# Shifting the moving operands of a decoder layer's matrix products by 48 bytes, and planning one small product later

## The chip, the cores and the metric

The kernel runs as one program on 1 core of one Trainium2 chip. The metric is the time of one execution on the device in microseconds (us), lower is better. The kernel before takes 1654.64 us, the median of 3 runs that lie between 1654.36 and 1654.86 us.

## What is computed

The reference is one layer of a decoder with three parallel branches. A prompt of 256 tokens and 8 samples of 4 tokens each pass through the same weights, so the kernel treats them together as T = 288 columns. Cut to what matters here:

```
h = rms_norm(x, g_mix);  proj = h @ w_in            # 2048 -> 10752 columns
u = u_lin * sigmoid(u_gate)                          # branch A: causal depthwise convolution, LayerNorm, swish
y_conv = swish(layer_norm(conv31(u))) @ w_conv_out
q, k = rms_norm(q_sb), rms_norm(k_sb)                # branch B: 8 heads of 128, stick-breaking attention
y_sb = stick_breaking(q, [past_k, k], [past_v, v]) @ w_sb_out
y_mem = softmax_attention(rms_norm(q_mem), mem_k, mem_v) @ w_mem_out    # branch M: 4 heads
x = x + (g_A*y_conv + g_B*y_sb + g_M*y_mem) @ w_o    # g_*: sigmoid gates out of proj
x = x + square(relu(rms_norm(x, g_mlp) @ w_up)) @ w_down                # 2048 -> 8192 -> 2048
```

All inputs are float32. The keys and values of the memory and of the new tokens are returned too.

## The kernel before

**Layout.** Activations lie with features on the 128 partitions and the 288 tokens along the free dimension, so a tensor of 2048 features is 16 tiles of 128x288. A weight is the stationary operand of a product, an activation tile the moving one, and a sum over the features builds up in one bank of PSUM (the memory into which TensorE writes).

**Three products for one.** The type `float32r` holds a rounded float32. To keep the precision, weights and activations are each split into a high part and a low part, both `float32r`: ScalarE (ACT) casts the weights (L302), VectorE (DVE) subtracts to get the low part (L313). One 128x128 block of weights then costs three products of 288 columns: high weight by high and by low activation, low weight by high activation. `products` (L490) writes them in pieces of 6; all go through `chunk` (L482), so nearly all of TensorE's work has the line L484. There are 11,712 such products, called *main products* here. The weights come in 504 slabs of 128x1024 floats (24 main products each) that SyncE's queue (SP) loads in order.

**Stages.** First the keys and values of the prompt's memory (`mem_products`, L537: there the weights are the moving operand, 512 columns wide), then the columns of `w_in` for the convolution (`conv_products`), the 4 memory heads, the 8 stick-breaking heads (key, query, value of each), gates and branch projections, `w_o`, and four rounds of `w_up` and `w_down`. Attention, convolution and the samples run on the other engines beside the main products, with small products of their own in between. The norms of a head need the sum of the squares over its 128 features: `head_norm` (L806) squares on ScalarE, adds the halves and splits on VectorE (L816, L820), and multiplies by a matrix of ones (L823). There are 20 such products. `sum_norm` (L443) does the same over 2048 features with two products (L439, L440).

**The order of the work.** Nothing is scheduled at run time. While the program is built, a planner (`Order`, L75) holds every step as an `Ask` with an engine, an estimated time, flags to wait for and buffers to take. It places the steps one by one at the earliest time it computes, by rank among those that are equally early. The estimates so set the order of the instructions in each engine's queue. `MM` (L176) is its estimate in us for one main product. `late` in an `Ask` puts a step that many us later than its inputs would allow. The engines then run their queues in that order and wait for semaphores.

**Where the operands lie.** The moving operands of the main products are in three pools. Pool `a` has 75 buffers of `APART` = 320 floats; an activation takes two of them, for its high and its low part (class `Acts`, L322), and uses the first 288 floats of each. From the fourth stage on, when the samples are done, the 9 buffers of `k4` (1024 floats, three operands in each, 320 apart) and the 8 of `s` (512 floats) become the fixed places of 16 operand pairs (`make_homes`, L1239). In the built program every one of the 11,712 moving operands starts 96 bytes past a multiple of 256; the blocks of weights start 32 bytes past a multiple of 64, and the weights that are moving operands at L537 also start 96 bytes past a multiple of 256. The convolution's first outputs lie in PSUM pools `pa` (3 banks) and `pm` (4 banks) and are held until the norm of x (`rx`, L434) is there.

Of the kernel before, what the change touches and what calls it, by code (L numbers as in the profile page):

```python
# [8 lines left out]
F32R = mybir.dt.float32r  # L9
# [5 lines left out]
P = 128  # L15
# [6 lines left out]
T = NP + NS  # L22
# [52 lines left out]
class Order:  # L75
# [31 lines left out]
    def give(self, pool, n=1):  # L107
        self.pools[pool] += [self.now.ready] * n
# [45 lines left out]
def dve(n, *flags, **take):  # L154
    return Ask("DVE", 0.18 + n / 920.0, flags, **take)


def act(n, *flags, **take):
    return Ask("ACT", 0.22 + n / 1200.0, flags, **take)
# [6 lines left out]
def pe(us, *flags, **take):  # L166
    return Ask("PE", us, flags, **take)


def sp(*flags, **take):  # L170
    return Ask("SP", 0.45, flags, **take)


APART = 320
VISIT, VISIT_K = 4, 8
MM = 0.1325  # L176
MM_MEM = 0.226


# [1 line left out]
def tile_decoder_step(ctx: ExitStack, tc: tile.TileContext, xT, memT, wall, cvec, kmat, ptab,  # L181
# [25 lines left out]
    def tl(p, shape, dt=F32):  # L207
        cnt[0] += 1
        return pools[p].tile(shape, dt, tag=p, name=f"{p}_{cnt[0]}")

    def bank(p):
        return tl(p, [P, 512])
# [46 lines left out]
    def col(c):  # L259
        return cv[:, c:c + 1]  # L260
# [9 lines left out]
    class Slab:  # L270
        def __init__(self, parts):
            self.parts = parts
            self.landed = [Flag() for _ in range(parts)]
            self.split = [Flag() for _ in range(parts)]
# [47 lines left out]
    class Acts:  # L322


        def __init__(self, n=T):
            self.h, self.l = tl("a", [P, APART], F32R)[:, :n], tl("a", [P, APART], F32R)[:, :n]
            self.flag = Flag()

    hm, hx = [None] * KT, [None] * KT
# [93 lines left out]
    def rsqrt_of(ss, n, dim, y, a, out):  # L423

        yield act(n)
        act_fn(LN_EXP, y, ss, AF.Ln, scale=1.0 / dim, bias=eps)
        yield act(n)
        act_fn(LN_EXP, y, y, AF.Exp, scale=-0.5)
        yield dve(n)
        nc.vector.scalar_tensor_tensor(a, ss, EPS * dim, y, op0=ALU.add, op1=ALU.mult)  # L430
        yield dve(n)
        nc.vector.scalar_tensor_tensor(a, a, -0.5 / dim, y, op0=ALU.mult, op1=ALU.mult)
        yield dve(n)
        nc.vector.scalar_tensor_tensor(out, a, 1.5, y, op0=ALU.add, op1=ALU.mult)  # L434

    def total(h, l, n):

        ss = bank("pa")[:, :n]
        nc.tensor.matmul(ss, ones_r, h, start=True, stop=False)  # L439
        nc.tensor.matmul(ss, ones_r, l, start=False, stop=True)  # L440
        return ss

    def sum_norm(acc, dim, out, flag, ready):  # L443
# [6 lines left out]
        nc.vector.tensor_sub(l, acc, h.bitcast(F32))  # L450
        yield pe(2 * MM, pa=1)
        ss = total(h, l, T)
# [37 lines left out]
    def products(ps, uses, acts, first=True, last=True, n=T):  # L490
# [6 lines left out]
        for i in range(0, len(todo), STEP):  # L497
            part = todo[i:i + STEP]
            yield pe(len(part) * MM, *sl.split, *{a.flag for _, _, a, _ in part})
            if i == 0 and first:  # L500
# [45 lines left out]
    def conv_products(evacs):  # L546
# [8 lines left out]
        for k2, o in turns:  # L555
# [9 lines left out]
            for i in range(2):  # L565
                todo.append((sl.l, slice(i * 512 + o * P, i * 512 + (o + 1) * P), "h", 2 * k2 + i))
            yield pe(6 * MM, *sl.split, hx_in[2 * k2], hx_in[2 * k2 + 1])
            if o == 0:
# [153 lines left out]
    def conv_norm():  # L722
# [7 lines left out]
        for turn in range(2):  # L730
# [5 lines left out]
            nc.vector.tensor_sub(l, acc, h.bitcast(F32))  # L736
            yield pe(2 * MM, pa=1)
            ss = total(h, l, T)
# [67 lines left out]
    def head_norm(ps, gcol, box, flag, p="pm"):  # L806

        yield dve(T, rx_done, t=4)
        raw, sq, hl, r = (tl("t", [P, T], F32R if i == 2 else F32) for i in range(4))
        nc.vector.tensor_mul(raw, ps, rx)  # L810
        give(p)
        yield act(T)
        nc.scalar.activation(sq, raw, AF.Square)
        yield dve(T)
        top, low = slice(0, P // 2), slice(P // 2, P)
        nc.vector.tensor_add(sq[top], sq[top], sq[low])  # L816
        yield act(T)
        nc.scalar.copy(hl[top], sq[top])
        yield dve(T)
        nc.vector.tensor_sub(hl[low], sq[top], hl[top].bitcast(F32))  # L820
        yield pe(MM, pa=1)
        ss = bank("pa")[:, :T]
        nc.tensor.matmul(ss, ones_r, hl, start=True, stop=True)  # L823
        yield from rsqrt_of(ss, T, HD, sq, r, r)
        give("pa")
        yield dve(T, a=1)
        out = tl("a", [P, T])
        nc.vector.scalar_tensor_tensor(out, raw, col(gcol), r, op0=ALU.mult, op1=ALU.mult)
        give("t", 4)
        box.append(out)  # L830
        done(flag)
# [45 lines left out]
    def mem_head(h):  # L877
        def evac(ps):
            box = []
            yield from head_norm(ps, C_GQM, box, Flag())  # L880
            q = box[0]
            if h == 0:
# [180 lines left out]
    def sb_key(h):  # L1063
        def evac(ps):
            box, ks[h] = [], Pair()
            yield from head_norm(ps, C_GK, box, Flag())
            add(store(oK[h], box[0]), 3)
            yield act(NS)
            nc.scalar.copy(kn[:, h, :], box[0][:, NP:])
            yield from split(ks[h], box[0][:, :NP], NP, k_made[h])  # L1070
            give("a")
        return evac

    def sb_query(h):
        def evac(ps):
            box, qs_[h] = [], Pair()
            yield from head_norm(ps, C_GQ, box, Flag())
            yield from split(qs_[h], box[0][:, :NP], NP, q_made[h])
            yield act(NS)
            nc.scalar.copy(qs[:, h, :], box[0][:, NP:])  # L1080
            give("a")
            done(qs_made[h])
        return evac
# [155 lines left out]
    def make_homes():  # L1239
        yield sp(*conv_done, *osb_in, k4=bufs["k4"], s=bufs["s"])  # L1240
        parts = []
        for _ in range(bufs["k4"]):
            x = tl("k4", [P, 1024], F32R)
            parts += [x[:, i * APART:i * APART + T] for i in range(3)]
        for _ in range(bufs["s"]):
            parts.append(tl("s", [P, 512], F32R)[:, :T])
        for j in range(KT):
            homes.append(Home(parts[2 * j], parts[2 * j + 1]))
        done(homes_in)
# [199 lines left out]
    with tc.manual_schedule():  # L1449
        add(loads(), 1.0)  # L1450
        add(cast_weights(), lambda: 0 if due(cast_at[0]) - order.free["ACT"] < 6.0 else 4.5)
        add(mem_norm(), 0.6)
        add(sum_norm(x_sum, D_MODEL, rx, rx_done, sums_x), 0.6)
        add(main(), 20.0)
        add(conv_norm(), 8.0)
        add(setup(), 1.0)
        add(read_pages(), 4.0)
        add(make_homes(), 1.0)
        order.run()
# [157 lines left out]
```

## Time and profile before

| | |
|---|---|
| median of 3 runs | 1654.64 us |
| the profiled execution | 1654.51 us |
| its span, first to last instruction | 1652.7 us |
| TensorE, matmuls (PE) | busy 1647.8 us, 12,786 instructions |
| TensorE, weight loads (PEld) | busy 1629.8 us |
| VectorE (DVE) | busy 991.7 us |
| ScalarE (ACT) | busy 737.8 us |
| GpSimd (POOL) | busy 140.1 us |
| DMA | 305.39 MB, mean 185 GB/s |

The profiled execution's own time is 1.8 us longer than its span and 0.13 us below the median. In a row of groups stand the line, the engine, the operation, the tiles (out<-in), shapes and count, then the busy time in us, the mean length of one in ns, and the idle time in front of them with what ended it. A matmul's length there is from its start to its end, and neighbours overlap, because they are pipelined; how fast they follow each other is read from the chain of waits, where a piece `849.22 800.29 PE pm L484 x6078` means: from 849.22 us on, for 800.29 us, 6078 matmuls one behind the other.

### The profile page before, as it was taken

To read this page: it belongs to the slowest core of one execution; us is meant where nothing else is said; L and a number is where in the kernel's file an instruction comes from. 1 tells how busy PE (TensorE), PEld (TensorE's weight loads), DVE (VectorE), ACT (ScalarE), POOL (GpSimd) and SP (SyncE) were. 2 spreads that over 40 slices of the span, in tenths; PEclk is the share of its full clock that TensorE was granted. 3 is DMA by queue.
4 is the path that set the end of the run, shared out by engine and by line. 5 is a ranking of instruction groups with operands and counts; after the bars stand their busy time and mean duration, and the time that the engine had idled before them with its cause. 6 is when DMAs were issued, how large, how long until landed. Compare 5 with 4: busy or idle time off the path is not lost.

```text
span 1652.7 us, 30966 instructions
## 1 busy us (share of the span) xinstructions
PE 1647.8 (100%) x12786; PEld 1629.8 (99%) x12786; DVE 991.7 (60%) x1471; ACT 737.8 (45%) x1070; POOL 140.1 (8%) x105
## 2 busy tenths in 40 slices
PE   9999999999999999999999999999999999999999
PEld 7999999999999999999999999999999999999999
DVE  7898888876677655565555544455444554455443
ACT  7846766644444534444443333333333333333332
POOL 0030000000000000001222200121001210022100
PEclk9999999999999999999999999999999999999999
DMA  9686466766755555546655555555555555555563
GB/s 326 221 182 250 140 206 206 263 244 232 259 163 165 169 172 167 170 153 208 188 173 166 167 167 166 167 166 170 165 171 166 168 167 166 166 166 166 178 189 100
DMA packets 107103, 305.39 MB, mean 185 GB/s; under 512 B 19922, under 2 KB 29522, under 8 KB 106962
## 3 DMA queue, kind: packets, MB, share of 16 engines
q1 hardware_dynamic: 106818, 303.39, 58.3%
q8 instruction: 100, 1.64, 0.4%
q14 instruction: 41, 0.34, 0.1%
q10 hardware_dynamic: 144, 0.02, 0.0%
HBM read 297.05 MB, written 6.32 MB: 184 GB/s over the span
## 4 chain that ended last, share of the span: by engine, by line
PE 99%; DVE 1%; issue 0%; POOL 0%; POOLq 0%
PE pm L484 92%; PE pm L537 3%; PE pa L484 1%; PE pl L1013 1%; PE pl L1186 0%; PE pa L850 0%; PE pa L851 0%; PE pa L849 0%; DVE a L715 0%; DVE wl L313 0%; PE pl L1029 0%; PE pa L1405 0%; PE pa L823 0%; DVE t L820 0%; PE pa L1140 0%
## 5 line engine op out<-in xcount | busy, mean ns | idle before, releaser
L302 ACT CAST wh<-wr 128x1024 fp32r<-128x1024 f32 (+1 forms) x520 | 529.7, 1021 | 656.8 <-PE pm L484 597.2
L484 PE MATMUL pm<-a,wh 128*128 128x288 f32 x5184 | 746.6, 294 | 0.0
L313 DVE TENSOR_TENSOR wl<-wr,wh 128x1024 fp32r<-128x1024 f32 (+1 forms) x520 | 616.3, 1188 | 190.9 <-ACT wh L302 189.8
L484 PEld LDWEIGHTS pm<-a,wh 128*128 128x128 f32 x5184 | 703.9, 188 | 1.3 <-issue 1.2
L484 PE MATMUL pm<-a,wl 128*128 128x288 f32 x2592 | 403.0, 294 | 0.0
L484 PEld LDWEIGHTS pm<-a,wl 128*128 128x128 f32 x2592 | 362.2, 188 | 1.1 <-issue 1.0
L484 PE MATMUL pm<-k,wh 128*128 128x288 f32 x2160 | 310.6, 294 | 0.0
L484 PEld LDWEIGHTS pm<-k,wh 128*128 128x128 f32 x2160 | 293.4, 188 | 0.0
L484 PE MATMUL pm<-k,wl 128*128 128x288 f32 x1120 | 173.6, 294 | 0.0
L484 PEld LDWEIGHTS pm<-k,wl 128*128 128x128 f32 x1120 | 156.4, 188 | 0.0
L1342 POOL TENSOR_TENSOR t<-t 128x288 f32<-128x288 f32 x64 | 96.6, 1510 | 608.5 <-DVE t L1339 608.5
L1356 DVE TENSOR_TENSOR a<-a,pm 128x288 f32<-128x288 f32 x64 | 29.1, 455 | 125.3 <-PE pm L484 125.3
L1339 DVE SCALAR_TENSOR_TENSOR t<-pm,r 128x288 f32<-128x288 f32 x64 | 29.3, 458 | 95.5 <-PE pm L484 95.5
L1345 ACT CAST k<-t 128x288 fp32r<-128x288 f32 x56 | 24.2, 433 | 116.5 <-POOL t L1342 116.5
L1258 DVE TENSOR_TENSOR t<-pm,rx 128x288 f32<-128x288 f32 x48 | 22.0, 458 | 78.5 <-PE pm L484 78.5
L484 PE MATMUL pm<-s,wh 128*128 128x288 f32 x400 | 65.7, 294 | 0.0
L715 DVE SCALAR_TENSOR_TENSOR a<-a,cv,a 128x256 f32<-128x256 f32 x120 | 59.6, 496 | 1.4
L484 PEld LDWEIGHTS pm<-s,wh 128*128 128x128 f32 x400 | 57.2, 188 | 0.0
L1328 POOL TENSOR_TENSOR t<-t,t 128x288 f32<-128x288 f32 x15 | 21.4, 1423 | 420.4 <-ACT t L1325 420.4
L1347 DVE TENSOR_TENSOR k<-t,k 128x288 fp32r<-128x288 f32 x52 | 23.7, 458 | 51.3 <-ACT k L1345 51.3
L537 PE MATMUL pm<-wh,a 128*128 128x512 f32 x128 | 35.0, 395 | 0.0
L484 PE MATMUL pm<-s,wl 128*128 128x288 f32 x160 | 34.0, 294 | 0.0
(214 smaller groups left out, 784.8 us busy)
## 6 DMA issues: line engine op xcount, KB each, us to landing
wr<-in_wall SPq DMA_DIRECT2D x488, 512.0 KB, 3.6
wr<-in_wall SPq DMA_DIRECT2D x32, 256.0 KB, 5.2
k<-in_kpool SPq DMA_DIRECT2D x32, 256.0 KB, 6.0
k<-in_vpool SPq DMA_DIRECT2D x32, 256.0 KB, 6.7
k<-in_mkc SPq DMA_DIRECT2D x8, 512.0 KB, 7.9
k<-in_mvc SPq DMA_DIRECT2D x8, 512.0 KB, 6.1
t<-in_xT SPq DMA_DIRECT2D x16, 144.0 KB, 3.8
out_yT<-a SPq DMA_DIRECT2D x16, 144.0 KB, 1.8
```

The source lines that it names most:

```text
L302: nc.scalar.copy(sl.h[:, c], sl.raw[:, c])
L313: nc.vector.tensor_sub(sl.l[:, c], sl.raw[:, c], sl.h[:, c].bitcast(F32))
L484: nc.tensor.matmul(ps, w, a, start=(first and i == 0), stop=(last and i == len(todo) - 1))
L537: nc.tensor.matmul(ps[m], y[:, m * P:(m + 1) * P], z[:, w], start=(k == 0 and j < 2), stop=(k == KT - 1 and j in (4, 5)))
L715: nc.vector.scalar_tensor_tensor(c[:, :NP], up[:, k:k + NP], w, c[:, :NP], op0=ALU.mult, op1=ALU.add)
L1258: nc.vector.tensor_mul(g, ps, rx)
L1328: nc.gpsimd.tensor_add(sq_sum[0], sq_sum[0], res[0])
L1339: nc.vector.scalar_tensor_tensor(r, ps, 0.0, r2, op0=ALU.max, op1=ALU.mult)
L1342: nc.gpsimd.tensor_mul(r, r, r)
L1345: nc.scalar.copy(a.h, r)
L1347: nc.vector.tensor_sub(a.l, r, a.h.bitcast(F32))
L1356: nc.vector.tensor_add(x1[j], x1[j], ps)
```

## The change

Three edits.

- The operands of pools `a`, `k4` and `s` begin `AHEAD` = 12 floats, 48 bytes, further inside their buffers. In pool `a` this holds for operands of 288 columns; the memory's operands of 256 columns, which are stationary, stay. 12 + 288 floats fit in the 320 of a buffer, and no buffer moves. In the built program all 11,712 moving operands now start 144 bytes past a multiple of 256; weights, the operands of L537, `t` buffers and PSUM stay where they were.
- The planner's estimate of a main product is 0.131 us in place of 0.1325.
- The product of a head's squares (L823) gets `late=1.5`.

```
-MM = 0.1325
+AHEAD = 12
+MM = 0.131
...
         def __init__(self, n=T):
-            self.h, self.l = tl("a", [P, APART], F32R)[:, :n], tl("a", [P, APART], F32R)[:, :n]
+            c = slice(AHEAD, AHEAD + n) if n == T else slice(0, n)
+            self.h, self.l = tl("a", [P, APART], F32R)[:, c], tl("a", [P, APART], F32R)[:, c]
...
         nc.vector.tensor_sub(hl[low], sq[top], hl[top].bitcast(F32))
-        yield pe(MM, pa=1)
+        yield pe(MM, pa=1, late=1.5)
...
             x = tl("k4", [P, 1024], F32R)
-            parts += [x[:, i * APART:i * APART + T] for i in range(3)]
+            parts += [x[:, AHEAD + i * APART:AHEAD + i * APART + T] for i in range(3)]
         for _ in range(bufs["s"]):
-            parts.append(tl("s", [P, 512], F32R)[:, :T])
+            parts.append(tl("s", [P, 512], F32R)[:, AHEAD:AHEAD + T])
```

The two planner edits change the order of the instructions on every engine, up to the end of attention. The number of TensorE's instructions is the same, and so is the order of the main products among themselves; the small products come at other places between them. Lines of the changed kernel are 1 higher from the old L175 on and 2 higher from the old L327 on, so that L484, L823 and L439 become L486, L825 and L441.

On TensorE, where the first of the 20 products of squares stands. `pm_1675` is the bank that sums up for the third memory head, `a_` are its activations, `wh_` and `wl_` high and low weights, `ones_r` the matrix of ones, `t_1603` the squares. Before:

```order
L484 MATMUL pm_1675<-a_417,wh_1558 128x288
L484 MATMUL pm_1675<-a_418,wh_1558 128x288
L823 MATMUL pa_1696<-t_1603,ones_r 128x288
L484 MATMUL pm_1675<-a_450,wh_1558 128x288
L484 MATMUL pm_1675<-a_451,wh_1558 128x288
```

and after:

```order
L486 MATMUL pm_1674<-a_473,wh_1551 128x288
L486 MATMUL pm_1674<-a_250,wl_1577 128x288
L486 MATMUL pm_1674<-a_267,wl_1577 128x288
L486 MATMUL pm_1674<-a_285,wl_1577 128x288
L486 MATMUL pm_1674<-a_382,wl_1577 128x288
L486 MATMUL pm_1674<-a_399,wl_1577 128x288
L486 MATMUL pm_1674<-a_417,wl_1577 128x288
L486 MATMUL pm_1674<-a_450,wl_1577 128x288
L486 MATMUL pm_1674<-a_472,wl_1577 128x288
L825 MATMUL pa_1710<-t_1599,ones_r 128x288
L486 MATMUL pm_1674<-a_488,wh_1588 128x288
```

It stood in the middle of the slab's high weights, behind 492 main products. Now it stands behind the slab's low weights, behind 504, so 12 main products later.

On TensorE, where the two products of the sum over x's squares stand. `pa_711` and `pm_807` are banks of the first convolution products, `pa_1122` takes the sum, `pm_1159` is the bank of the next convolution tile. Before:

```order
L484 MATMUL pa_711<-a_694,wl_1030 128x288
L439 MATMUL pa_1122<-t_1083,ones_r 128x288
L440 MATMUL pa_1122<-t_1084,ones_r 128x288
L484 MATMUL pm_807<-a_670,wh_1006 128x288
L484 MATMUL pm_807<-a_671,wh_1006 128x288
```

and after:

```order
L486 MATMUL pm_1159<-a_549,wh_1049 128x288
L486 MATMUL pm_1159<-a_611,wh_1049 128x288
L486 MATMUL pm_1159<-a_612,wh_1049 128x288
L441 MATMUL pa_1220<-t_1118,ones_r 128x288
L442 MATMUL pa_1220<-t_1119,ones_r 128x288
L486 MATMUL pm_1159<-a_614,wh_1049 128x288
L486 MATMUL pm_1159<-a_615,wh_1049 128x288
L486 MATMUL pm_1159<-a_618,wh_1049 128x288
```

The sum stood behind 180 main products and stands behind 222, inside the next convolution tile; four transposes of the memory's keys (L631, now L633) have taken its old place.

## The prediction

> **What bounds the kernel now.** I read the profile's first part, then the stretches by stage, then the chain of waits. The first part says which engine is never idle:
>
> ```profile
> span 1652.7 us, 30966 instructions
> PE 1647.8 (100%) x12786; PEld 1629.8 (99%) x12786; DVE 991.7 (60%) x1471; ACT 737.8 (45%) x1070; POOL 140.1 (8%) x105
> ```
>
> PE's 100% only means that matmuls overlap without a hole. The stretches by stage show whether another engine comes near it somewhere, and the granted clock:
>
> ```profile
> core 0: us, PE busy (x) PEld busy (x) DVE busy (x) ACT busy (x) POOL busy (x), PEclk, DMA share, GB/s
> 60.00:125.00 65.00, 64.59 (x492) 64.36 (x491) 58.19 (x93) 37.40 (x63) 12.96 (x7) 1.00 0.75 186
> 125.00:400.00 275.00, 275.00 (x2386) 269.64 (x2384) 227.26 (x436) 164.66 (x321) 5.72 (x6) 1.00 0.66 227
> 530.00:1650.00 1120.00, 1119.49 (x8503) 1119.26 (x8501) 563.53 (x688) 429.56 (x507) 117.97 (x79) 1.00 0.55 168
> ```
>
> The clock is at 1.00 everywhere, DMA has room, and VectorE is at 58.19 of 65 us (90%) only in the convolution's stage, and at 50% in the last two thirds. So TensorE sets the end, and the question is at which pace its products follow each other. The chain tells that:
>
> ```profile
> 373.35 26.86 PE pm L484 x204
> 530.58 318.37 PE pm L484 x2418
> 849.08 0.14 PE pa L440
> 849.22 800.29 PE pm L484 x6078
> 1649.53 0.45 DVE a L1356
> ```
>
> 800.29/6078 = 131.67 ns for one main product, with nothing between; 318.37/2418 and 26.86/204 give the same 131.67. The pieces hold operands from pool `a` alone (373 us) and from `a`, `k4` and `s` (849 us), high and low, in all banks. The pace doesn't depend on any of that. The count of main products is the sum of eight groups:
>
> ```profile
> L484 PE MATMUL pm<-a,wh 128*128 128x288 f32 x5184 | 746.6, 294 | 0.0
> L484 PE MATMUL pm<-a,wl 128*128 128x288 f32 x2592 | 403.0, 294 | 0.0
> L484 PE MATMUL pm<-k,wh 128*128 128x288 f32 x2160 | 310.6, 294 | 0.0
> L484 PE MATMUL pm<-k,wl 128*128 128x288 f32 x1120 | 173.6, 294 | 0.0
> L484 PE MATMUL pm<-s,wh 128*128 128x288 f32 x400 | 65.7, 294 | 0.0
> L484 PE MATMUL pm<-s,wl 128*128 128x288 f32 x160 | 34.0, 294 | 0.0
> L484 PE MATMUL pa<-a,wh 128*128 128x288 f32 x64 | 11.2, 297 | 0.0
> L484 PE MATMUL pa<-a,wl 128*128 128x288 f32 x32 | 6.8, 294 | 0.0
> ```
>
> Together 11,712, and 11,712 x 131.67 ns = 1542 us of the 1652.7. One nanosecond per product is 11.7 us.
>
> **How much of 131.67 ns belongs to columns.** The products at L537 are 512 columns wide and also start 96 bytes past a multiple of 256. In the timeline of TensorE their weights repeat every six:
>
> ```profile
> 40.83 0.61 PE L537 MATMUL pm<-wl,a 128*128 128x512 f32 x2
> ...
> 48.99 0.61 PE L537 MATMUL pm<-wl,a 128*128 128x512 f32 x2
> ```
>
> Six groups of 6 lie between, 36 products in 48.99 - 40.83 = 8.16 us, so 226.67 ns each. From 288 to 512 columns the pace grows by 95.0 ns, 0.424 ns per column. 288 columns are worth 122.1 ns; 9.5 ns of a main product are a fixed cost, alike for both widths. That is 111 us in all, and it is the most that a better start of the operand can save.
>
> **The change part by part.** *The shift by 48 bytes.* It adds no instruction. Its direct effect on TensorE no row of before shows, since all main operands start alike. Bounds: all of the fixed cost could go (-111 us); upward, the same 9.5 ns could come a second time (+111 us). Between these ends I go by how far inside a block of memory the operand starts, if a read takes whole blocks and passes the columns ahead of the operand at the pace of columns. That is an assumption. The starts are 96 bytes past a multiple of 256 before and 144 after, so the columns ahead are, for blocks of 16 bytes, 0 and 0; of 32, 0 and 4; of 64, 8 and 4; of 128, 24 and 4; of 256, 24 and 36. 24 columns cost 10.2 ns, more than the 9.5 ns that there are, so blocks of 128 and 256 fit the rows badly. Of 64, 8 columns are 3.4 ns and fit in. I take 64: 4 columns less, 4 x 0.424 = 1.70 ns, 11,712 x 1.70 = 19.9 us saved. It is the size nearest to the fixed cost that does not overshoot it; 16 and 32 would leave the whole 9.5 ns to something else, which may be.
>
> [...]
>
> The engines that write the shifted operands are hidden. In the last two thirds these are, for one:
>
> ```profile
> L1345 ACT CAST k<-t 128x288 fp32r<-128x288 f32 x56 | 24.2, 433 | 116.5 <-POOL t L1342 116.5
> L1347 DVE TENSOR_TENSOR k<-t,k 128x288 fp32r<-128x288 f32 x52 | 23.7, 458 | 51.3 <-ACT k L1345 51.3
> ```
>
> At twice their length they would add some 24 us to each engine, in a stage of 1120 us where VectorE is idle for 556. I put this at nothing. If TensorE gets 1.3% faster, VectorE's share in 60:125 rises from 90 to 91%: no new bound.
>
> *The product of squares later.* One of the 20 held TensorE up:
>
> ```profile
> 112.56 3.48 POOL L702 TENSOR_TENSOR k<-a,cv 128x992 f32<-128x992 f32 x1 [6.54 <-DVE a L688]
> ...
> 114.05 2.31 DVE L820 TENSOR_TENSOR t<-t,t 64x288 fp32r<-64x288 f32 x1
> ...
> PE pa L823 <- DVE t L820: 0.4, 1, 0.4
> ```
>
> VectorE's split took 2.31 us here, beside a GpSimd operation, and TensorE waited 0.4 us. 12 main products more ahead of L823 are 12 x 0.13167 = 1.58 us, which covers it: -0.4 us. What it costs: ScalarE's L225 waits longer for L823, and a head holds its four `t` buffers about 1.5 us longer. The head's results are wanted many main tiles later, so nothing of that shows on TensorE unless a small product behind it comes late too; one such wait would be about as long, 0.4 us. I set the two against each other: 0, with -0.4 to +1.5 us as bounds.
>
> *The planner's estimate.* It moves the sum over x's squares behind 42 more main products, 5.5 us. Behind that sum wait the first outputs of the convolution, which hold their banks:
>
> ```profile
> 74.34 0.13 PE pa L440
> ...
> 76.51 0.46 DVE L434 SCALAR_TENSOR_TENSOR rx<-t,t 128x288 f32<-128x288 f32 x1
> ...
> 78.79 0.45 DVE L658 TENSOR_TENSOR a<-pm,rx 128x288 f32<-128x288 f32 x1
> ```
>
> From L440 to the first `pm` bank given back it is 79.24 - 74.34 = 4.9 us, 37 main products. The first tile that needs such a bank starts behind 288 main products (192 of the first eight slabs, two tiles of 48). 222 + 37 = 259, so 29 products, 3.8 us, of slack are left where there were 71. It costs nothing; with the cover gone it would cost the lateness itself, a microsecond or two, once.
>
> *Sum.* 1654.51 (this execution) - 19.9 = 1634.6; the median lies 0.13 higher: **1634.8 us**.
>
> **The rivals.** *The start doesn't matter* (the fixed cost is something else, or blocks of 16 bytes are what counts). For it: the pace is the same 131.67 in every piece, and nothing in the trace ties it to an address. Against it: 9.5 ns fixed need a cause. Time: 1654.6 less the 0.4 at L823 = 1654.2. The Trainium skill (SBUF — State Buffer, Specifications) speaks of cachelines of 16 bytes; 96 and 144 are both multiples of 16, so by it this rival holds; no run here shows the size of a line.
>
> *Slower: blocks of 32 bytes.* 96 is 3 x 32, 144 is 4.5 x 32: the old start meets the boundary and the new one misses it by 4 columns. Every main product then costs 1.70 ns more, +19.9 us: 1674.5. It decides as soon as the boundary that counts is one that 96 meets. Against it: then the 9.5 ns are there without any columns ahead.
>
> *Large blocks.* 128 bytes: 20 columns less, 8.48 ns, -99.3 us: 1555.3. 256 bytes: 12 columns more, 5.09 ns, +59.6 us: 1714.2. Against both stands 10.2 over 9.5 ns.
>
> That the shift misses some operands is no rival: in the built program all 11,712 have moved.
>
> **How the numbers follow.** Chances: 0.62 for my forecast, 0.20 for no matter, 0.10 for 32 bytes, 0.05 and 0.03 for 128 and 256. Even if the mechanism is right, its price is uncertain by half: 2 to 6 columns, 9.9 to 29.8 us, so 1644.7 to 1624.8 is the forecast's own range. The range takes in that and the case of no change with its +1.5 us: 1624 to 1656. Left out are the large blocks and the 32 bytes, 0.18. A difference of 0.2%, 3.3 us, is about what a measurement of this kernel can tell from no change. Faster: 0.62 + 0.05 = 0.67; same 0.20; slower 0.10 + 0.03 = 0.13.
>
> **What would show it.** In the profile after, the long last pieces of the chain should come out at 131.67 - 1.70 = 129.97 ns per product (x6078: 789.9 us instead of 800.29), while L537 keeps 226.67 ns. PE's wait for L820 should be gone, and no wait for a bank should appear between 75 and 95 us. The forecast is wrong if the pace is still 131.67 (nothing gained), if it is above (the new start is the worse one), or if the pace falls and the span doesn't, because the small products or the splits of the weights now hold TensorE up before 530 us.

## The result, and the profile after

The changed kernel takes 1639.84 us (1639.37 to 1640.01, 4 runs) against 1654.74 us before (1654.36 to 1654.86, 4 runs) on the same chip: a ratio of 0.9911, 95% interval 0.9899 to 0.9922. 14.9 us are gained of the 19.9 that were forecast. The profile's first part:

```profile
span 1637.6 us, 30963 instructions
PE 1633.0 (100%) x12786; PEld 1615.7 (99%) x12786; DVE 992.2 (61%) x1471; ACT 739.3 (45%) x1070; POOL 138.9 (8%) x105
```

TensorE is still the bound, and the other engines have the busy time that they had. Where the gain lies, the chain of waits tells. Start, length, and number of main products (now L486) of its long pieces:

```profile
79.92 37.37 PE pm L486 x282
...
439.71 84.27 PE pm L486 x636
...
546.77 297.18 PE pm L486 x2286
...
844.22 790.16 PE pm L486 x6078
```

The last two are 130.0 ns per product (297.18/2286, 790.16/6078), almost exactly the 129.97 of the forecast. But the first two are 132.5 ns (37.37/282, 84.27/636): *slower* than the 131.67 that stood in every piece before. The same instructions on operands placed alike now have two paces, and each piece keeps one of them from end to end. The last 6078 products gain 800.29 - 790.16 = 10.1 us, the 2286 before them 2286 x 1.67 ns = 3.8 us. The 3348 main products ahead of these gain only 1.2 us together: the piece of 2286 starts at 546.77, and before, its first product stood 132 products into the piece that began at 530.58, at 530.58 + 132 x 0.13167 = 547.96.

The other things foretold are there. The list of what TensorE waits for has one row left, the start, and the wait at the product of squares is gone:

```profile
PE pa L1407 <- POOL eps L234: 1.3, 1, 1.3
```

The piece from 79.92 us on runs without a break, so no bank was missing after the later sum. The 512-column products kept their pace (36 in 8.16 us):

```profile
40.39 0.61 PE L539 MATMUL pm<-wl,a 128*128 128x512 f32 x2
...
48.55 0.61 PE L539 MATMUL pm<-wl,a 128*128 128x512 f32 x2
```

### The profile page after: what moved, and what is told of

Same layout as the page of the kernel before. It is cut to its first block, busy times and chain, and to the rows that moved or that the text cites. A ratio compares the mean times of both kernels' runs of the same rounds, so it can differ in the third digit from the quotient of the medians.

```text
span 1637.6 us, 30963 instructions
## 1 busy us (share of the span) xinstructions
PE 1633.0 (100%) x12786; PEld 1615.7 (99%) x12786; DVE 992.2 (61%) x1471; ACT 739.3 (45%) x1070; POOL 138.9 (8%) x105
## 4 chain that ended last, share of the span: by engine, by line
PE 100%; POOL 0%; DVE 0%; issue 0%; POOLq 0%
PE pm L486 93%; PE pm L539 3%; PE pa L486 1%; PE pl L1015 1%; PE pl L1188 0%; PE pa L852 0%; PE pa L853 0%; PE pa L851 0%; PE pl L1031 0%; PE pa L1407 0%; PE pa L825 0%; PE pa L1142 0%; PE pa L906 0%; PE pa L1139 0%; PE pa L1141 0%; PE pa L1106 0%
## 5 line engine op out<-in xcount | busy, mean ns | idle before, releaser
L486 PE MATMUL pm<-a,wh 128*128 128x288 f32 x5184 | 742.3, 293 | 0.0
L486 PEld LDWEIGHTS pm<-a,wh 128*128 128x128 f32 x5184 | 699.7, 188 | 1.3 <-issue 1.2
L486 PE MATMUL pm<-a,wl 128*128 128x288 f32 x2592 | 398.6, 293 | 0.0
L486 PEld LDWEIGHTS pm<-a,wl 128*128 128x128 f32 x2592 | 359.8, 188 | 0.0
L486 PE MATMUL pm<-k,wh 128*128 128x288 f32 x2160 | 306.8, 292 | 0.0
L486 PEld LDWEIGHTS pm<-k,wh 128*128 128x128 f32 x2160 | 290.2, 188 | 0.0
L486 PE MATMUL pm<-k,wl 128*128 128x288 f32 x1120 | 171.6, 292 | 0.0
L486 PEld LDWEIGHTS pm<-k,wl 128*128 128x128 f32 x1120 | 155.0, 188 | 0.0
L486 PE MATMUL pm<-s,wh 128*128 128x288 f32 x400 | 65.0, 293 | 0.0
L486 PEld LDWEIGHTS pm<-s,wh 128*128 128x128 f32 x400 | 56.6, 188 | 0.0
L486 PE MATMUL pm<-s,wl 128*128 128x288 f32 x160 | 33.8, 293 | 0.0
```

Of the source, the lines that this page charges most:

```text
L486: nc.tensor.matmul(ps, w, a, start=(first and i == 0), stop=(last and i == len(todo) - 1))
```

## The experiments

Theory A is the prediction's: the pace falls by the columns that lie ahead of the operand in a block of 64 bytes. Four rivals are named in the expectations: B, the distance between the moving operand and the weights counts; C, the planner's edits do it; D, what stands just ahead of a run picks one of several paces; E, only the start of the moving operand counts. F is D's counterpart: the program's order as a whole fixes the pace. All kernels but those with extra products compute the same as the changed one; the extra products' results are not used.

**The two halves of the change, each by itself.** The shift alone:

```
-MM = 0.131
+MM = 0.1325
...
-        yield pe(MM, pa=1, late=1.5)
+        yield pe(MM, pa=1)
```

> The shift by 48 bytes alone, with the planner's numbers of before. Theory A (the start of the moving operand inside a block of 64 bytes sets the pace): the long last pieces of the chain stay at 130.0 ns per main product, the time is within 2 us of the changed kernel's 1639.8. Rival C (the new order of the instructions does it): the pace is back at 131.67 ns, the time about 1654.

1654.66 us, ratio 1.0 (0.999 to 1.0009): nothing is gained. The planner's edits alone (`AHEAD = 0`):

> The planner's two edits alone, operands at the old place (96 past 256). Theory A: pace 131.67 ns, time 1654.2, at most 0.4 us off the kernel before for the wait at the product of squares. Rival C: about 1640.

1653.97 us, ratio 0.9995 (0.9985 to 1.0005): nothing to speak of either. Neither half is worth anything that can be told from no change, and both together are worth 14.9 us. The chain of the shift alone says how:

```profile
444.86 67.57 PE pm L486 x510
...
530.13 314.35 PE pm L486 x2418
...
844.73 805.35 PE pm L486 x6078
```

805.35/6078 = 132.5 ns and 314.35/2418 = 130.0. The two paces are back, but the last run, the longest, took the slow one. Its difference to the changed kernel, 805.35 - 790.16 = 15.2 us, accounts for the 14.8 us between the two times. The planner's edits alone have 131.67 ns in every long piece, the last among them:

```profile
848.92 800.28 PE pm L486 x6078
```

So the shift replaces one pace (131.67) by two (130.0 and 132.5), and the planner's edits only change which run gets which. A explains neither the two paces nor the 132.5.

What kind of product stands ahead of the last run can't be what differs here. In both kernels it is the same two products of a sum (L441, L442), behind a run at 130.0 ns, and in the built programs the last 8366 products follow in the same order over weights at the same addresses. Only the buffers of the moving operands and the PSUM banks are in part others, and so is everything before. Which of these differences gives 130.0 in one kernel and 132.5 in the other, no run shows.

**Starting on a multiple of 64.** `AHEAD = 8`:

> The changed kernel with 32 bytes in place of 48, so that the moving operands start on a multiple of 64 (128 past 256). Theory A (columns ahead of the operand in a block of 64 bytes are passed at 0.42 ns each): no column ahead, 8 columns less than before, pace 131.67 - 3.4 = 128.3 ns, the last 6078 products in 780 us, time about 1622. Rival B (what counts is the distance in bytes between the moving operand and the weights that are loaded at the same time, both 32 past 64 before): 32 is another distance than 48, and the pace can be anything, 130.0 to 133.

1673.1 us, ratio 1.0111 (1.0091 to 1.0131), and the last run is

```profile
857.54 810.42 PE pm L486 x6078
```

133.33 ns: the start that A holds to be the best is slower than every pace seen so far. Then every buffer 32 bytes further with `AHEAD = 0`, by a small buffer ahead of all others:

```
+    open_pool("pad", 1).tile([P, 8], F32, name="pad")
     cpool = open_pool("const", 1)
```

> Every buffer moved by 32 bytes, weights too, with no shift inside the buffers: moving operands and weights both start on a multiple of 64, and their distance is that of before. The planner's numbers are those of the changed kernel. Theory A: no column ahead, pace 128.3 ns, time about 1622. Rival B (only the distance to the weights counts): pace 131.67 ns as before, time about 1654.

1653.84 us, ratio 0.9995 (0.9985 to 1.0005), and

```profile
848.41 800.28 PE pm L487 x6078
```

131.67 ns, as before the change. The moving operands start on a multiple of 64 in both kernels, and the paces are 133.33 and 131.67; with the distance to the weights unchanged the pace is unchanged. A has fallen, and so have all its sizes of block, since the two kernels' moving operands start at the same place in a block of any size up to 256 bytes (128 past a multiple of 256). B stands, though the second kernel moves every other buffer along with the weights.

**Other distances.** `AHEAD = 4` and `AHEAD = 16`, each run once, as is the kernel behind them:

> The changed kernel with 16 bytes in place of 48. Theory B now (the distance between moving operand and weights, counted within 64 bytes, sets which paces are possible: 0 gave 131.67 ns, 32 gave 133.33, 48 gave 130.0 or 132.5): 16 is a new distance, with a pace or paces of its own between 129 and 134 ns. Theory A (columns ahead in a block of 64 bytes; 12 columns here) would give 131.67 + 1.7 = 133.4 ns, one pace.

> The changed kernel with 64 bytes in place of 48. Theory B: the distance is 0 again within 64 bytes, so one pace, 131.67 ns, in all long pieces and a time of 1654. Rival (the distance counts within 128 or 256 bytes, or the absolute start does): another pace than 131.67.

16 bytes: 1653.46 us beside 1655.07 for the kernel before; the last run at 131.67 ns (800.28 us), three shorter ones, of 144, 78 and 60 products, at 130.0 from their ninth product on. 64 bytes: 1654.32 us; two paces again, 84.09/636 = 132.2 and 131.67 ns:

```profile
440.97 84.09 PE pm L486 x636
...
849.06 800.28 PE pm L486 x6078
```

A distance of 0 had 131.67 alone, so distances don't repeat after 64 bytes: that part of B was wrong. Then the weights 16 bytes further, with the operands at their old place (meant as a distance of -16):

```
-AHEAD = 12
+AHEAD = 0
...
-                sl.h = tl("wh", [P, SLAB], F32R)
+                sl.h = tl("wh", [P, SLAB + 16], F32R)[:, 4:4 + SLAB]
...
-            sl.l = tl("wl", [P, SLAB], F32R)
+            sl.l = tl("wl", [P, SLAB + 16], F32R)[:, 4:4 + SLAB]
```

> Moving operands at their old place (32 past a multiple of 64), the split weights 16 bytes further (48 past a multiple of 64), the planner's numbers of the changed kernel. The distance from weights to operand is -16, which is 48 within 64 bytes. Theory B: main products at 130.0 or 132.5 ns. Rival E (only the start of the moving operand counts): 131.67 ns, about 1654.

1656.44 us; the last run takes 800.74 us, 131.74 ns. That is neither B's 130.0 or 132.5 nor quite the 131.67 of E: with the weights' place it moves a little, by 0.07 ns. But this run doesn't have one distance. Its weights' buffers lie 4160 bytes apart in place of 4096, so in the built program a quarter of the products each has weights 48, 112, 176 and 240 past a multiple of 256, where the kernel before has 96 throughout. Since distances don't repeat after 64 bytes, it can't test B, and against E it has only these 0.07 ns.

**Who picks the pace.** Extra products ahead of each of the 128 tiles of the last two matrices, their weights 32 columns of the ones, 16 to 128 columns wide in turn:

```
+    def kick():
+        yield pe(0.05, pa=1)
+        n = 16 * (kicks[0] % 8 + 1)
+        kicks[0] += 1
+        nc.tensor.matmul(bank("pa")[:32, :n], ones_r[:, :32], ones_r[:, :n], start=True, stop=True)
+        give("pa")
...
+                yield from kick()
                 yield from main_tile(hh, up_tile(u, f))
...
+                yield from kick()
                 yield from main_tile(u, down_tile(j, c == D_FF // D_MODEL - 1))
```

> The changed kernel with one small extra product (32 columns of weights, 16 to 128 columns wide, in turn; its result is not used) ahead of each of the 128 main tiles of the last two matrices. Theory D (at a distance of 48 a run of main products holds one of two paces, and what stands just ahead of the run decides which): the tiles run at 130.0 or at 132.5 ns, some of each, and the width ahead decides, so the time is 1639.8 plus some 5 us for the extra products plus up to 15. Rival F (the pace hangs on buffers or on the planner's order of the whole program): all tiles at 130.0 ns as without them, about 1645.

1660.29 us in its one run (the extra products cost more than expected, about 0.1 us each). TensorE's timeline around two of them, of 32 and of 48 columns:

```profile
893.97 0.18 PE L1417 MATMUL pa<-ones_r 128*32 128x32 f32 x1
...
897.20 2.24 PE L486 MATMUL pm<-a,wh 128*128 128x288 f32 x16
899.28 1.20 PE L486 MATMUL pm<-a,wl 128*128 128x288 f32 x8
900.32 0.18 PE L1417 MATMUL pa<-ones_r 128*32 128x48 f32 x1
...
903.61 2.28 PE L486 MATMUL pm<-a,wh 128*128 128x288 f32 x16
905.73 1.22 PE L486 MATMUL pm<-a,wl 128*128 128x288 f32 x8
```

Behind 32 columns 16 products take 899.28 - 897.20 = 2.08 us, 130.0 ns each; behind 48 columns 905.73 - 903.61 = 2.12 us, 132.5. So it goes on: in the 127 tiles with nothing else between, all behind 16, 48 and 96 columns ran at 132.5, all behind 32, 64, 80, 112 and 128 at 130.0, without an exception. In this kernel the pace is picked anew when a run begins, and held until something breaks it. F has fallen as far as it says that the order and the buffers alone fix the pace; that they have no part in it isn't shown.

**The gain without the planner's edits.** The shift alone (first experiment) with one extra product of 32 columns, ahead of the third tile of `w_up`:

```
+                if c == 0 and f == 2:
+                    yield from kick(32)
                 yield from main_tile(hh, up_tile(u, f))
```

> The shift by 48 bytes with the planner's numbers of before, and a single small extra product (32 columns wide, result not used) ahead of the third tile of w_up. Theory D (what stands ahead of a run decides its pace, and 32 columns set 130.0 ns): the last 6048 products go from 132.5 to 130.0 ns, 15.1 us saved, about 1639.7 in place of 1654.7. Rival F (the planner's order of the whole program decides, not the moment): still 132.5 ns and 1654.7.

1640.02 us, ratio 0.991 (0.9894 to 0.9927). A product of no use makes the kernel 14.6 us faster than the shift alone. The chain around it:

```profile
844.23 3.98 PE pm L486 x30
848.21 0.02 PE pa L1413
848.23 786.35 PE pm L486 x6048
```

3.98/30 = 132.7 ns ahead of it, 786.35/6048 = 130.0 behind. Up to the extra product, and again behind it, TensorE's products are those of the shift alone in the built programs, with all operands at the same addresses. The same product in the kernel before, at distance 0 (one run):

> The kernel before with the same single extra product at the same place. Theory D: at the old distance of 0 all long runs have the one pace of 131.67 ns, so the extra product changes nothing, 1654.7. If the extra product helps by itself, whatever the distance: about 1640 to 1645.

1654.81 us beside 1654.83, and still 131.67 ns:

```profile
853.40 796.42 PE pm L484 x6048
```

With one pace there is nothing to pick.

**More distances.** The extra products of above, and `w_down`'s operands 80, 96, 112 and 16 bytes inside their buffers in the four rounds:

```
+        for ahead in (AHEAD, 20, 24, 28, 4):
+            at = [x[:, o + ahead:o + ahead + T] for x, o in parts]
+            rounds.append([Home(at[2 * j], at[2 * j + 1]) for j in range(KT)])
...
-            a = homes[f]
+            a = rounds[c + 1][f]
```

> The changed kernel with extra products of 16 to 128 columns ahead of each tile of the last two matrices, and the operands of w_down in its four rounds 80, 96, 112 and 16 bytes inside their buffers (w_up's stay at 48). Theory D with paces by distance: the 16 tiles of each round show the paces that this distance allows. 16 bytes: 130.0 and 131.67 ns as seen before. 80, 96 and 112: if the distance counts within 64 bytes, 80 like 16, 96 like 32 (133.33), 112 like 48 (130.0 and 132.5); if not, other numbers. The time itself tells nothing.

It ran once. The chain, one tile of 48 products from each of the four rounds in this order (a piece holds the slower start behind its extra product too, so its length by its count is more than its pace):

```profile
951.46 6.38 PE pm L486 x48
...
1149.87 6.42 PE pm L486 x48
...
1355.12 6.48 PE pm L486 x48
...
1561.86 6.42 PE pm L486 x48
```

Over the last 32 products of each tile the starts are 131.1 ns apart at 80 bytes, 131.7 or 133.3 at 96, 133.3 to 135.1 at 112, and 131.7 at 16. So 80 is not like 16, 96 not like 32, and 112 far from 48. No distance tried has a pace below 130.0.

The tiles of `w_up` in this run are at a distance of 48 with the extra products of the experiment above, and there the widths don't always pick what they picked before. In the third round the tiles behind 16 and behind 32 columns stand in the chain as

```profile
1246.50 6.34 PE pm L486 x48
1252.85 0.01 PE pa L1415
1252.86 6.45 PE pm L486 x48
```

By their last 32 products these are 130.0 behind 16 columns and 132.5 behind 32, the other way round. Six of the 63 undisturbed tiles of `w_up` break the rule of the widths, all among the first six behind a round of `w_down`. So what came earlier counts too.

**An attempt to beat both.** The changed kernel with all buffers 32 bytes further and extra products of 32 columns at three places:

```
+            if br == 1 and j0 in (0, 8):
+                yield from kick(32)
...
+                if c == 0 and f == 2:
+                    yield from kick(32)
```

> The changed kernel with every buffer, the weights' too, 32 bytes further (the moving operands then start 48 past a multiple of 64, at the same distance of 48 from the weights), and three extra products of 32 columns: ahead of the first and of the ninth tile of the second branch's gates and ahead of the third tile of w_up. Theory B with D (the distance decides which paces there are, what stands ahead of a run decides which of them it takes): the paces are 130.0 and 132.5 ns as in the changed kernel, the last 6048 products at 130.0; some 490 products of the second branch go from 132.5 to 130.0, 1.2 us, against three extra products of 0.12 us: about 1639, at best faster than the changed kernel by a microsecond. Rival E (the start of the moving operand by itself decides): other paces than 130.0 and 132.5.

1659.51 us, ratio to before 1.0028 (1.0018 to 1.0039): *slower than before*.

```profile
440.13 19.08 PE pm L487 x144
459.21 0.02 PE pa L1416
459.23 64.06 PE pm L487 x492
...
523.54 10.93 PE pm L487 x84
534.47 0.02 PE pa L1416
534.49 11.23 PE pm L487 x84
...
545.98 302.90 PE pm L487 x2286
...
853.04 0.02 PE pa L1416
853.06 801.47 PE pm L487 x6048
```

The paces are 132.5 and 130.0, as at the same distance without the move, and none of E's other paces appears: B holds, E doesn't. The first extra product did its work (19.08/144 = 132.5 ahead of it, 64.06/492 = 130.2 behind, its own start included). The second did the opposite: 84 products ahead of it were at 130.0 (10.93/84 = 130.1, start included), the 84 behind it take 0.30 us longer, at 132.5 once under way. The third, of the width that picked 130.0 in the shift alone, picked 132.5. And the run of 2286, which was at 130.0 in the changed kernel, is at 132.5 here though the same two products, with another PSUM bank, stand ahead of it in both. Width alone is no recipe. Against the changed kernel the two runs lose (2286 + 6048) x 2.5 ns = 20.8 us, the 492 gain 1.2, which makes 1639.8 + 19.6 = 1659.4.

## Why the prediction was right, and where its steps failed

**The bound and the count** held: TensorE sets the end, 11,712 main products, 11.7 us per nanosecond; every time above follows from the paces of the long runs.

**The price of the shift** came out in size, 1.67 ns for 1.70 in the runs at 130.0, and so did the sign. **Its mechanism** failed. The step was that a read passes the columns ahead of the operand in a block of 64 bytes. With no column ahead the pace was 133.33 (32 bytes) or 131.67 (all buffers moved), where the step gives 128.3. What the runs put in its place: the place of the moving operand relative to the buffers that are read with it, the weights by all likelihood, gives one or more steady paces. The agreement of 130.0 with 129.97 was chance, and the time near the forecast was luck: the same shift also gave 132.5 ns in its longest run and no gain. The range of 1624 to 1656 held both outcomes. That the 9.5 ns are a fixed cost which a better start can save stayed an assumption; no place tried saved more than 1.67 of them. The rival of blocks of 32 bytes falls in the same way: of two starts that miss no boundary, one gave 133.33. "The start doesn't matter", and with it the reading by which only lines of 16 bytes (the size that the Trainium skill, SBUF — State Buffer, Specifications, gives) count, falls too: starts that are all multiples of 16 gave paces from 130.0 to 135.1. The large blocks fall with the step itself, by the two kernels with one start and two paces.

**The step "the planner's edits are worth nothing"** failed, and it is the one that decides. I looked for waits that the new order adds or removes, found none that mattered, and that was true: by itself the new order is worth at most some 0.7 us, which its interval doesn't tell from nothing. Yet at this distance the order decides which of the two paces each long run takes, 130.0 or 132.5 ns. With the order of before the same shift gives 1654.66 us, no gain at all.

**The missing 5 us** are the runs at 132.5 ns in attention and the branches: 3348 products that were to gain 1.70 ns each, 5.7 us, gained 1.2.

**The wait at the product of squares** went, as said. The shift alone, without the later planning, shows it again, at 0.7 us:

```profile
PE pa L825 <- DVE t L822: 0.7, 1, 0.7
```

Shown are: two paces at this distance, that one small product can flip the pace of the run behind it, and that the paces stay when all buffers move together (at distances of 0 and 48 bytes). That the weights, and no other buffer, are the far end of the distance is argued and not shown: the one run that moves the weights alone mixes four distances. Open is what inside TensorE makes the paces. That the reads of the moving operand and of the weights meet would fit; no run looks inside. Open too is what picks a pace when a run begins: the width of the product ahead counts, but the same width gave either pace, and so did the same two products of a sum.

## What to carry to other kernels

Where one engine runs back to back, read its pace from long pieces of the chain (length by count), stage by stage, before and after: two edits that are worth nothing apart can be worth 15 us together, and a pace shows it while the busy shares and the waits hardly do. Try operand places relative to weights, and test each with a small disturbance ahead of the long runs: a gain that a useless product of 0.1 us can give or take is not a property of the shift alone. Keep such a gain under watch, since any later edit of the order may flip it.

## What the runs showed of the hardware

- Products of 288 columns behind each other held paces of 130.0, 131.1, 131.67, 132.2, 132.5, 133.33 and 135.1 ns, at full granted clock, with no wait in the profile, with the moving operand 0 to 112 bytes past its old place and the weights where they were (131.1 and 135.1 in tiles of 48 products alone).
- At a distance of 48 bytes two paces exist, 130.0 and 132.5 ns; a run of 6078 products kept one of them to its end.
- A single product with 32 columns of weights, 32 columns wide, ahead of a run of 6048 took 14.6 us off at a distance of 48 bytes, and nothing (1654.81 us beside 1654.83) at a distance of 0.
